# A hybrid decoder step: dt's columns and the sample's scores in strips, value products in pairs, the conv state in six pieces

## The chip, the cores and the metric

One NeuronCore of a Trainium2 chip runs the whole program. TensorE multiplies matrices into PSUM, VectorE and ScalarE work on rows of up to 128 partitions, GpSimd (POOL) and SyncE (SP) mainly issue DMAs, and 16 DMA engines move data between HBM and the on-chip memory. The metric is the time of one execution on the device, in microseconds (us), as the median of several runs.

## The reference

One layer of a decoder handles 256 prompt tokens and 8 sample tokens with the same weights: 264 columns in all.

```python
h = rmsnorm(x)
q, k, v, z, xbc, dt, qm, g = split(h @ w_in)      # 2048 -> 13856 features; dt has 32
A = sliding_window_attention(q, k, v)             # 16 heads, 4 key heads, window 128
B = mamba2_ssd(conv(xbc), z, softplus(dt + bias)) # 32 heads, state 128, conv over 4 tokens
M = attention(qm, memory)                         # 4 heads, 256 memory tokens
x = x + (sig(g_A)*(A @ up_A) + sig(g_B)*(B @ up_B) + sig(g_M)*(M @ up_M)) @ w_out
x = x + (silu(n @ w_gate) * (n @ w_up)) @ w_down  # n = rmsnorm(x)
```

A sample token attends to 128 cached keys of its own and to its own new key. Its convolution uses three cached tokens (`state_conv`, 8 x 3 x 3072). Keys, values and states are also outputs. Everything is float32.

## The kernel before

Activations lie with features on the partitions: a feature tile is 128 features by 264 tokens, and the 2048 features of h are 16 tiles. Weights come in units of 128 x 1024 numbers. For each unit SP issues a DMA into `raw`, ScalarE rounds it to `hi` in the matrix format float32r (L181, in `split`), VectorE takes the rest `lo = raw - hi` (L182), and TensorE multiplies (L160, in `mm`). A product in full precision is three matrix products: `hi` with the high part of the activation (`hh`), `hi` with its low part (`hl`), `lo` with the high part. An ordinary group gives 512 output features: eight units of 24 products each. `feed(i)` asks for the DMAs four units ahead and splits three units ahead.

The units stand in a list, and the loop at the end of the kernel runs through it. After each unit it lets two queues of side work go on: `side` with a credit of 1.0 for a unit, `slow` with 0.75. A task is a generator, and each `yield` gives the price of the step it has done; `yield None` ends the turn. `side` does its tasks in order: memory norm, `prep_x`, `consts`, memory attention, `swa_keys` (W1), `swa` (W), the convolutions of B and C, `task_dt`, and the four SSD groups. `side.drain(name)` finishes a task at once; `x_group(0)`, the unit group behind dt's, drains W first.

This is only the order of tracing. The tile framework then plans the order of each engine with a simulated timeline: what was traced earlier has precedence, and what is not ready in the simulation lets later work pass. On the chip each engine follows the planned order, and semaphores stop it where data is late.

Tiles come from pools. `sps` gives one of three PSUM tiles for side work, `dps` one of five for the groups; `t1`, `t2`, `t4` give SBUF tiles of 264, 512 and 1056 numbers, four each.

The places that the change touches:

- `consts` (L498 to L549) makes constants. The conv state comes as three DMAs of 24 rows (8 tokens x 3) by 1024 channels into `sc` (L535), and 24 transposes of 24 x 128 turn it into `scT`. VectorE multiplies by the conv weights and sums into `pre` (L541, L544). L518 makes a mask `m16` of row number modulo 16.
- `swa` (L821) is the window attention. It makes `qmask`, the sample's queries with zeros where key head and query head differ (L838 to L843), in the column order token, head pair, half, head. For each of four (block, pair of key heads) it computes scores and softmax, then the values: a piece is 128 keys for two query heads of each of two key heads, four transposes into `pT` (L923), a ScalarE copy into `pTa` (L925), and two float32 products into `po`, one into partitions 0 to 63 and one into 64 to 127 (L929). The later block has four pieces for a pair of key heads, the first block two.
- The sample scores follow (L938 on). For two tokens at a time four transposes turn the cached keys into `kcT`; for each token and pair of key heads one product with the keys stationary and 8 columns of `qmask` moving goes into `sTs`. VectorE copies it, a transpose puts it into `sS` with a row for each token and head, and one more product adds the new key's score. Then come softmax, transposes into `pSt`, a copy into `pTS`, and the value products `poS`, in strips of 32 output columns.
- `dt_group` (L1337) computes the 32 features of dt in two units, each with eight feature tiles of 128 weight columns: dt's 32 and 96 of the next part, which aren't used. It has 48 products into `pdt`.
- `task_dt` (L1106) transposes dt (`dtT`), adds the bias, and makes softplus, running sums and decay factors.

Of the kernel before, what the change touches and what calls it, by code (L numbers as in the profile page):

```python
# [18 lines left out]
P = 128  # L19
# [58 lines left out]
def tile_hybrid_decoder_step(  # L78
# [80 lines left out]
    def mm(out, lhsT, rhs, start=True, stop=True):  # L159
        nc.tensor.matmul(out, lhsT=lhsT, rhs=rhs, start=start, stop=stop)  # L160
# [91 lines left out]
    def do_split(n):  # L252
        if n < state["split"]:
            return
        raw = raws.pop(n)
        hi = wp.tile([P, 1024], F32R, tag="hi", name=nm("hi"), bufs=3)
        lo = wp.tile([P, 1024], F32R, tag="lo", name=nm("lo"), bufs=3)
        if units[n].get("perm"):
            for k in range(2):
                v = [t[:, k * 512:(k + 1) * 512].rearrange("p (r a d) -> p a r d", r=4, a=2) for t in (hi, lo)]  # L260
                s = raw[:, k * 512:(k + 1) * 512].rearrange("p (a r d) -> p a r d", a=2, r=4)
                split(v[0], v[1], s)
        else:
            split(hi, lo, raw)
        parts[n] = (hi, lo)
        state["split"] = n + 1
# [228 lines left out]
    def consts():  # L495
# [22 lines left out]
        V.tensor_reduce(m16, ident.rearrange("p (b h) -> p h b", h=16), axis=AX.X, op=ALU.add)  # L518
# [14 lines left out]
        for h in range(3):  # L533
            sc = t4("sc")[0:24, 0:1024]
            nc.gpsimd.dma_start(sc, state_conv[0, :, :, h * 1024:(h + 1) * 1024].rearrange("b k c -> (b k) c"))  # L535
            ps = sps("scT")
            for c in range(8):
                tr(ps[:, c * 24:(c + 1) * 24], sc[:, c * P:(c + 1) * P])
            tm = t1("tm")
            w3 = cw.rearrange("p (k c) -> p c k", k=4)[:, h * 8:(h + 1) * 8, 0:3]  # L540
            V.tensor_tensor(tm[:, 0:192].rearrange("p (c b k) -> p c b k", c=8, b=NS),  # L541
                            ps[:, 0:192].rearrange("p (c b k) -> p c b k", c=8, b=NS),
                            w3.unsqueeze(2).broadcast_to([P, 8, NS, 3]), op=ALU.mult)
            V.tensor_reduce(pre[:, h * 8:(h + 1) * 8, :], tm[:, 0:192].rearrange("p (c b k) -> p c b k", c=8, b=NS),  # L544
                            axis=AX.X, op=ALU.add)
            yield 1
# [274 lines left out]
    def swa():  # L821
# [16 lines left out]
        qm_ = t1("qmask")[:, 0:P].rearrange("p (b v a r) -> p b v a r", b=NS, v=2, a=2)  # L838
        V.memset(qm_.rearrange("p b v a r -> p (b v a r)"), 0.0)
        for a in range(2):  # L840
            rows = slice(a * 64, a * 64 + 64)
            for kvp in range(2):
                V.tensor_copy(qm_[rows, :, kvp, a, :].rearrange("p b r -> p r b"), q[rows, 4 * kvp:4 * kvp + 4, NP:NT])  # L843
        qmf = qm_.rearrange("p b v a r -> p (b v a r)")
# [31 lines left out]
        for blk in (1, 0):  # L876
            nk = 256 if blk else 128
            for kvp in range(2):
# [38 lines left out]
                for rp in range(2):  # L917
                    for kb in range(nk // P):
                        p2 = sps("pT")
                        for a in range(2):  # L920
                            for r2 in range(2):
                                o = (2 * a + r2) * P
                                tr(p2[:, o:o + P], s[a][:, 2 * rp + r2, kb * P:(kb + 1) * P])  # L923
                        pT = t2("pTa")
                        act(pT, p2, AF.Copy)  # L925
# [10 lines left out]
        pT_s = sps("sTs")  # L936
        kcs = {}
        for b in range(NS):  # L938
            if b % 4 == 0:
                kc = next(other_loads).rearrange("p (b c) -> p b c", b=4)  # L940
            if b % 2 == 0:
                ps = sps("kcT")
                for j in range(2):
                    for c in range(2):
                        tr(ps[:, (2 * j + c) * P:(2 * j + c + 1) * P], kc[:, b % 4 + j, c * P:(c + 1) * P])
                kcT = t2("kcT")
                act(kcT, ps, AF.Copy, scale=gq_c)
            for c in range(2):
                o = b * 16 + c * 8
                mm(pT_s[:, o:o + 8], kcT[:, (2 * (b % 2) + c) * P:(2 * (b % 2) + c + 1) * P], qmf[:, o:o + 8])  # L950
            yield 0.1
        sT = t1("sTsb")[:, 0:P]
        V.tensor_copy(sT, pT_s[:, 0:P])
        pkn = t1("pkn")[:, 0:P].rearrange("p (b v e) -> p b v e", b=NS, v=2)
        V.tensor_tensor(pkn, qm_.rearrange("p b v a r -> p b v (a r)"),
                        kT[:, :, NP:NT].rearrange("p v b -> p b v").unsqueeze(3).broadcast_to([P, NS, 2, 8]), op=ALU.mult)
# [27 lines left out]
        mm(ps[:, P:2 * P], ones, dg)  # L984
        pT = t1("pTS")[:, 0:256]
        V.tensor_copy(pT, ps[:, 0:256])
# [118 lines left out]
    def task_dt():  # L1105
# [34 lines left out]
        xs = tiny("dts", NS)[0:32]  # L1140
        V.tensor_scalar(xs, raw[:, NP:NT], hcol[:, 0:1], None, op0=ALU.add)
# [195 lines left out]
    def dt_group():  # L1337
        st = {}

        def loads(u):  # L1340
            def f(raw):
                return [(raw.rearrange("p (k n) -> p k n", k=8),
                         w_in[0, 8 * u * P:8 * (u + 1) * P, C_DT:C_DT + P].rearrange("(k p) n -> p k n", p=P))]
            return f

        def prod(u):
            def f(hi, lo):
                if u == 0:
                    st["ps"] = dps("pdt")[:, 0:NT]
                for k in range(8):  # L1350
                    kk = 8 * u + k
                    wh, wl = hi[:, k * P:(k + 1) * P], lo[:, k * P:(k + 1) * P]
                    mm(st["ps"], wh, hh(kk), start=kk == 0, stop=False)
                    mm(st["ps"], wh, hl(kk), start=False, stop=False)
                    mm(st["ps"], wl, hh(kk), start=False, stop=kk == KT - 1)
            return f

        def after():
            raw = t1("dtraw")[0:32]
            act(raw, st["ps"][0:32], AF.Copy)  # L1360
# [3 lines left out]
        for u in range(2):  # L1364
            units.append(dict(loads=loads(u), prod=prod(u), after=after if u else None))
# [310 lines left out]
```

## Time and profile before

| | |
|---|---|
| median of 3 runs | 1933.8 us (1928.26, 1933.8, 1938.96) |
| profiled execution | 1933.54 us, its span 1931.8 us |
| mean granted TensorE clock | 0.999 |
| DMA | 402.92 MB, mean 209 GB/s |
| costliest group, TensorE | the projection `pin`, 3 x 1728 products of 128 x 264 |

A line of the time order holds the start in us from the span's beginning, the time taken, the engine, the line of the kernel, the operation, what is written from what (out<-in), the shape (for a product, rows of contraction x output rows, then the moving operand) and how many instructions stand in it; in brackets follows the idle time before it and what ended it. PE is TensorE's products, PEld its weight loads. Matrix products overlap, so the times of single ones don't add up; from one start to the next does. A line of the waits holds who waited, for whom, the total, how many times, and the longest. In a list by tile three numbers are the shortest, median and longest time of one in ns.

### The profile page before, as it was taken

To read this page: it belongs to the slowest core of one execution; us is meant where nothing else is said; L and a number is where in the kernel's file an instruction comes from. 1 tells how busy PE (TensorE), PEld (TensorE's weight loads), DVE (VectorE), ACT (ScalarE), POOL (GpSimd) and SP (SyncE) were. 2 spreads that over 40 slices of the span, in tenths; PEclk is the share of its full clock that TensorE was granted. 3 is DMA by queue.
4 is the path that set the end of the run, shared out by engine and by line. 5 is a ranking of instruction groups with operands and counts; after the bars stand their busy time and mean duration, and the time that the engine had idled before them with its cause. 6 is when DMAs were issued, how large, how long until landed. Compare 5 with 4: busy or idle time off the path is not lost.

```text
span 1931.8 us, 37682 instructions
## 1 busy us (share of the span) xinstructions
PE 1905.2 (99%) x15401; PEld 1857.1 (96%) x15401; DVE 1168.0 (60%) x2246; ACT 969.7 (50%) x1423; POOL 133.6 (7%) x269
## 2 busy tenths in 40 slices
PE   8999999999999999999999999999999999999998
PEld 6899999989999999999999999999999999999998
DVE  5665577665568878588455666555445555445553
ACT  6654456665657685646444444444334434334443
POOL 3010101001002122011000000000000000000000
PEclk9999999999999999999999999999999999999999
DMA  8686758767668789778656656665556665566653
GB/s 278 209 264 214 212 171 297 223 190 234 200 181 279 241 228 301 250 262 282 180 189 213 222 182 176 184 182 180 183 178 183 178 185 177 184 177 183 176 192 126
DMA packets 191956, 402.92 MB, mean 209 GB/s; under 512 B 13891, under 2 KB 16242, under 8 KB 191648
## 3 DMA queue, kind: packets, MB, share of 16 engines
q1 hardware_dynamic: 169856, 324.13, 54.6%
q0 software_dynamic: 21776, 76.33, 11.9%
q8 instruction: 120, 1.97, 0.4%
q14 instruction: 52, 0.43, 0.1%
q10 hardware_dynamic: 152, 0.07, 0.0%
HBM read 376.53 MB, written 26.22 MB: 208 GB/s over the span
## 4 chain that ended last, share of the span: by engine, by line
PE 87%; DMA 4%; issue 4%; DVE 3%; ACT 2%; POOL 1%; ACTq 0%; SPq 0%; POOLq 0%; DVEq 0%
PE pin L160 25%; PE pu L160 13%; PE pdn L160 13%; PE pg L160 13%; PE pus L160 5%; PE pout L160 5%; PE pmem L160 5%; DMA ring<-in_state_ssm_dram 2%; PE pum L160 1%; PE pua L160 1%; DVE lo L182 1%; DMA ld<-in_cache_mem_v_dram 1%; DVE ring L1295 1%; DMA ld<-in_cache_mem_k_dram 1%; ACT hi L181 0%
## 5 line engine op out<-in xcount | busy, mean ns | idle before, releaser
L182 DVE TENSOR_TENSOR lo<-raw,hi 128x1024 fp32r<-128x1024 f32 (+1 forms) x626 | 746.8, 1196 | 599.4 <-ACT hi L181 598.2
L181 ACT ACTIVATE hi<-raw 128x1024 fp32r<-128x1024 f32 (+1 forms) x626 | 646.0, 1036 | 835.0 <-PE pin L160 191.8
L160 PE MATMUL pin<-hh,hi 128*128 128x264 f32 x1728 | 489.3, 287 | 0.6 <-DVE sig L1439 0.5
L160 PE MATMUL pin<-hl,hi 128*128 128x264 f32 x1728 | 489.0, 286 | 0.0
L160 PE MATMUL pin<-hh,lo 128*128 128x264 f32 x1728 | 473.8, 285 | 1.8 <-DVE lo L182 1.8
L160 PEld LDWEIGHTS pin<-hh,hi 128*128 128x128 f32 x1728 | 325.4, 189 | 5.6 <-issue 3.6
L160 PEld LDWEIGHTS pin<-hl,hi 128*128 128x128 f32 x1728 | 325.5, 188 | 2.7 <-issue 2.4
L160 PEld LDWEIGHTS pin<-hh,lo 128*128 128x128 f32 x1728 | 317.3, 188 | 3.8 <-DVE lo L182 2.3
L160 PE MATMUL pdn<-fah,hi 128*128 128x264 f32 x704 | 199.7, 285 | 0.0
L160 PE MATMUL pdn<-fal,hi 128*128 128x264 f32 x704 | 199.4, 285 | 0.0
L160 PE MATMUL pu<-h2h,hi 128*128 128x264 f32 x704 | 199.4, 284 | 0.0
L160 PE MATMUL pu<-h2l,hi 128*128 128x264 f32 x704 | 199.3, 284 | 0.0
L160 PE MATMUL pg<-h2l,hi 128*128 128x264 f32 x704 | 199.1, 285 | 0.0
L160 PE MATMUL pg<-h2h,hi 128*128 128x264 f32 x704 | 198.4, 284 | 0.0
L160 PE MATMUL pdn<-fah,lo 128*128 128x264 f32 x704 | 197.0, 284 | 0.0
L160 PE MATMUL pu<-h2h,lo 128*128 128x264 f32 x704 | 196.6, 284 | 0.0
L160 PE MATMUL pg<-h2h,lo 128*128 128x264 f32 x704 | 196.1, 284 | 0.0
L160 PEld LDWEIGHTS pdn<-fah,hi 128*128 128x128 f32 x704 | 132.7, 189 | 0.1
L160 PEld LDWEIGHTS pu<-h2h,hi 128*128 128x128 f32 x704 | 132.7, 189 | 0.0
L160 PEld LDWEIGHTS pg<-h2h,hi 128*128 128x128 f32 x704 | 132.7, 188 | 0.0
L160 PEld LDWEIGHTS pdn<-fal,hi 128*128 128x128 f32 x704 | 132.6, 188 | 0.1
L160 PEld LDWEIGHTS pu<-h2l,hi 128*128 128x128 f32 x704 | 132.6, 188 | 0.0
(531 smaller groups left out, 2966.0 us busy)
## 6 DMA issues: line engine op xcount, KB each, us to landing
raw<-in_w_in_dram SPq DMA_DIRECT2D x218, 512.0 KB, 4.3
raw<-in_w_gate_dram SPq DMA_DIRECT2D x88, 512.0 KB, 3.7
raw<-in_w_up_dram SPq DMA_DIRECT2D x88, 512.0 KB, 3.9
raw<-in_w_down_dram SPq DMA_DIRECT2D x88, 512.0 KB, 4.2
raw<-in_w_mem_kv_dram SPq DMA_DIRECT2D x32, 512.0 KB, 4.5
raw<-in_w_up_ssd_dram SPq DMA_DIRECT2D x32, 512.0 KB, 4.2
raw<-in_w_out_dram SPq DMA_DIRECT2D x32, 512.0 KB, 4.4
ld<-in_cache_mem_k_dram POOLq DMA_DIRECT2D x16, 512.0 KB, 5.8
```

Of the source, the lines that this page charges most:

```text
L160: nc.tensor.matmul(out, lhsT=lhsT, rhs=rhs, start=start, stop=stop)
L181: act(hi, src, AF.Copy)
L182: V.tensor_tensor(lo, src, hi.bitcast(F32), op=ALU.subtract)
L1295: V.scalar_tensor_tensor(hb, bb[:, b], dx[:, b:b + 1], hb, op0=ALU.mult, op1=ALU.add)
```

## The change

- **dt**: one unit instead of two. Its DMA takes only the 32 columns of dt, for all 16 feature tiles (2048 pieces of 128 bytes). Nothing is split: ScalarE copies the 512 columns, and the products are plain float32. Feature tiles 4j to 4j + 3 go into four strips of 32 partitions of `pdt`, so that the strips' sum is dt. `mm` returns its instruction, and `tc.keep_in_program_order` pins each of these products behind the one traced before it on TensorE.
- **`task_dt`** sums the four strips with a matrix `sm` of ones at equal row number modulo 32, in place of the transposes, and takes the sample's columns the same way.
- **Value products**: the pieces go in pairs, eight transposes and two copies first, then the eight products, the later piece first, pinned.
- **Sample scores**: `qmask` has a new column order, which separates even and odd tokens. The keys of all tokens are transposed first (two `t4` tiles). Then 16 float32 products have 32 columns of masked queries (`wq`, VectorE copies) stationary and 128 keys moving, in four strips, four deep, pinned, straight into `sS`. The copy `sTs` and the transpose go. Copying `pTS` restores the old column order in four pieces.
- **Conv state**: four DMAs put six pieces of 96 rows by 128 channels into `sc`; six transposes, two multiplications and two sums follow.
- `m16` gets the new row order.

```diff
@@ -157,7 +157,7 @@
     def mm(out, lhsT, rhs, start=True, stop=True):
-        nc.tensor.matmul(out, lhsT=lhsT, rhs=rhs, start=start, stop=stop)
+        return nc.tensor.matmul(out, lhsT=lhsT, rhs=rhs, start=start, stop=stop)
@@ -255,7 +255,9 @@
         lo = wp.tile([P, 1024], F32R, tag="lo", name=nm("lo"), bufs=3)
-        if units[n].get("perm"):
+        if units[n].get("whole"):
+            act(hi.bitcast(F32)[:, 0:512], raw[:, 0:512], AF.Copy)
+        elif units[n].get("perm"):
@@ -515,7 +517,10 @@
         m16 = tiny("m16", 16)
-        V.tensor_reduce(m16, ident.rearrange("p (b h) -> p h b", h=16), axis=AX.X, op=ALU.add)
+        m2 = tiny("m2", 64)
+        V.tensor_tensor(m2, ident[:, 0:64], ident[:, 64:P], op=ALU.add)
+        V.tensor_reduce(m16.rearrange("p (v e) -> p v e", v=2), m2.rearrange("p (v b e) -> p v e b", v=2, b=4),
+                        axis=AX.X, op=ALU.add)
@@ -530,19 +535,19 @@
-        for h in range(3):
-            sc = t4("sc")[0:24, 0:1024]
-            nc.gpsimd.dma_start(sc, state_conv[0, :, :, h * 1024:(h + 1) * 1024].rearrange("b k c -> (b k) c"))
+        sc = t4("sc")[0:96, 0:768].rearrange("p (i n) -> p i n", i=6)
+        for c in range(4):
+            nc.gpsimd.dma_start(sc[24 * c:24 * c + 24],
+                                state_conv[0].rearrange("b k (i c n) -> c (b k) i n", c=4, n=P)[c])
+        for h in range(2):
             ps = sps("scT")
-            for c in range(8):
-                tr(ps[:, c * 24:(c + 1) * 24], sc[:, c * P:(c + 1) * P])
...
-                            axis=AX.X, op=ALU.add)
+            for i in range(3):
+                tr(ps[:, i * 96:(i + 1) * 96], sc[:, 3 * h + i])
+            tm = t2("tm")[:, 0:288].rearrange("p (c b k) -> p c b k", c=12, b=NS)
+            w3 = cw.rearrange("p (k c) -> p c k", k=4)[:, h * 12:(h + 1) * 12, 0:3]
+            V.tensor_tensor(tm, ps[:, 0:288].rearrange("p (c b k) -> p c b k", c=12, b=NS),
+                            w3.unsqueeze(2).broadcast_to([P, 12, NS, 3]), op=ALU.mult)
+            V.tensor_reduce(pre[:, h * 12:(h + 1) * 12, :], tm, axis=AX.X, op=ALU.add)
@@ -835,13 +840,16 @@
             tr(psT[:, t], ss[:, t * P:(t + 1) * P])
-        qm_ = t1("qmask")[:, 0:P].rearrange("p (b v a r) -> p b v a r", b=NS, v=2, a=2)
-        V.memset(qm_.rearrange("p b v a r -> p (b v a r)"), 0.0)
+        qmf = t1("qmask")[:, 0:P]
+        qm_ = qmf.rearrange("p (o v b e) -> p o v b e", o=2, v=2, b=4)
+        V.memset(qmf, 0.0)
             for kvp in range(2):
-                V.tensor_copy(qm_[rows, :, kvp, a, :].rearrange("p b r -> p r b"), q[rows, 4 * kvp:4 * kvp + 4, NP:NT])
-        qmf = qm_.rearrange("p b v a r -> p (b v a r)")
+                for o in range(2):
+                    V.tensor_copy(qm_[rows, o, kvp, :, 4 * a:4 * a + 4].rearrange("p b r -> p r b"),
+                                  q[rows, 4 * kvp:4 * kvp + 4, NP + o:NT:2])
@@ -914,8 +922,10 @@
-                for rp in range(2):
-                    for kb in range(nk // P):
+                pieces = [(rp, kb) for rp in range(2) for kb in range(nk // P)]
+                for n in range(0, len(pieces), 2):
+                    pTs_ = []
+                    for rp, kb in pieces[n:n + 2]:
@@ -923,40 +933,46 @@
                         act(pT, p2, AF.Copy)
+                        pTs_.append(pT)
+                        yield 0.2
+                    for (rp, kb), pT in reversed(list(zip(pieces[n:n + 2], pTs_))):
                             kv = 2 * kvp + a
-                            mm(po[rows, 256 * rp:256 * rp + 256], v_tok[:, vb_, kv * 64:(kv + 1) * 64],
-                               pT[:, 256 * a:256 * a + 256], start=kb == 0, stop=kb == nk // P - 1)
-                        yield 0.4
+                            tc.keep_in_program_order(
+                                mm(po[rows, 256 * rp:256 * rp + 256], v_tok[:, vb_, kv * 64:(kv + 1) * 64],
+                                   pT[:, 256 * a:256 * a + 256], start=kb == nk // P - 1, stop=kb == 0))
-        pT_s = sps("sTs")
-        kcs = {}
-        for b in range(NS):
+        wq = t2("wq").rearrange("p (i s e) -> p i s e", i=4, s=4)
+        V.memset(wq.rearrange("p i s e -> p (i s e)"), 0.0)
+        for i in range(4):
+            V.tensor_copy(wq[:, i, :, 8 * i:8 * i + 8], qmf.rearrange("p (s b e) -> p s b e", s=4, b=4)[:, :, i])
+        kcT = [t4("kcT")[:, 0:1024].rearrange("p (i s k) -> p i s k", i=2, s=4) for _ in range(2)]
+        for b in range(0, NS, 2):
                 kc = next(other_loads).rearrange("p (b c) -> p b c", b=4)
-            if b % 2 == 0:
-                ps = sps("kcT")
...
-                        kT[:, :, NP:NT].rearrange("p v b -> p b v").unsqueeze(3).broadcast_to([P, NS, 2, 8]), op=ALU.mult)
+            ps = sps("kcT")
+            for j in range(2):
+                for c in range(2):
+                    tr(ps[:, (2 * j + c) * P:(2 * j + c + 1) * P], kc[:, b % 4 + j, c * P:(c + 1) * P])
+            act(kcT[b // 4][:, b // 2 % 2].rearrange("p s k -> p (s k)"), ps, AF.Copy, scale=gq_c)
+            yield 0.2
+        yield None
         ps = sps("sS")
-        tr(ps[:, 0:P], sT)
-        mm(ps[:, P:P + 1], pkn.rearrange("p b v e -> p (b v e)"), onec)
+        for i in (3, 2, 1, 0):
+            for st_ in range(4):
+                tc.keep_in_program_order(mm(ps[32 * st_:32 * st_ + 32, 0:P], wq[:, i, st_], kcT[i // 2][:, i % 2, st_],
+                                            start=i == 3, stop=i == 0))
+        pkn = t1("pkn")[:, 0:P].rearrange("p (o v b e) -> p o v b e", o=2, v=2, b=4)
+        for v in range(2):
+            V.tensor_tensor(pkn[:, :, v], qm_[:, :, v],
+                            kT[:, v, NP:NT].rearrange("p (b o) -> p o b", o=2).unsqueeze(3).broadcast_to([P, 2, 4, 8]),
+                            op=ALU.mult)
+        mm(ps[:, P:P + 1], pkn.rearrange("p o v b e -> p (o v b e)"), onec)
@@ -982,8 +998,12 @@
         mm(ps[:, P:2 * P], ones, dg)
         pT = t1("pTS")[:, 0:256]
-        V.tensor_copy(pT, ps[:, 0:256])
+        for w in (0, P):
+            for o in range(2):
+                V.tensor_copy(pT[:, w:w + P].rearrange("p (b o v e) -> p o v b e", b=4, o=2, v=2)[:, o],
+                              ps[:, w:w + P].rearrange("p (o v b e) -> p o v b e", o=2, v=2, b=4)[:, o])
@@ -1108,9 +1128,16 @@
         x = tiny("dtx", 64)
+        sm = t1("dtsum")[:, 0:P]
+        V.tensor_reduce(sm[:, 0:32], ident.rearrange("p (a h) -> p h a", a=4), axis=AX.X, op=ALU.add)
+        V.tensor_copy(sm[:, 32:P].rearrange("p (a h) -> p a h", a=3), sm[:, 0:32].unsqueeze(1).broadcast_to([P, 3, 32]))
         for t in range(2):
-            tr(ps[:, t * 32:(t + 1) * 32], raw[:, t * P:(t + 1) * P])
+            mm(ps[:, t * 32:(t + 1) * 32], raw[:, t * P:(t + 1) * P], sm[:, 0:32])
+        mm(ps[:, 64:64 + NS], sm, raw[:, NP:NT])
+        xs = tiny("dts", NS)[0:32]
+        V.tensor_scalar(xs, ps[0:32, 64:64 + NS], hcol[:, 0:1], None, op0=ALU.add)
@@ -1137,8 +1164,6 @@
-        xs = tiny("dts", NS)[0:32]
-        V.tensor_scalar(xs, raw[:, NP:NT], hcol[:, 0:1], None, op0=ALU.add)
@@ -1335,34 +1360,29 @@
     def dt_group():
-        st = {}
-        def loads(u):
...
-            return f
+        def loads(raw):
+            return [(raw[:, 0:512].rearrange("p (k n) -> p k n", k=KT),
+                     w_in[0, :, C_DT:C_DT + 32].rearrange("(k p) n -> p k n", p=P))]
+        def prod(hi, lo):
+            ps = dps("pdt")[:, 0:NT]
+            w = hi.bitcast(F32)
+            for j in range(4):
+                for x in (hh, hl):
+                    for q in range(4):
+                        k = 4 * j + q
+                        tc.keep_in_program_order(mm(ps[32 * q:32 * q + 32], w[:, 32 * k:32 * k + 32], x(k).bitcast(F32),
+                                                    start=j == 0 and x is hh, stop=j == 3 and x is hl))
+            ssd["dtps"] = ps
         def after():
-            raw = t1("dtraw")[0:32]
-            act(raw, st["ps"][0:32], AF.Copy)
+            raw = t1("dtraw")
+            act(raw, ssd["dtps"], AF.Copy)
-        for u in range(2):
-            units.append(dict(loads=loads(u), prod=prod(u), after=after if u else None))
+        units.append(dict(loads=loads, prod=prod, after=after, whole=True))
     mg = {}
```

More of the change, by code (lines that the diff above doesn't have):

```diff
@@ L531, in consts @@
         yield 3
-        for h in range(3):
-            sc = t4("sc")[0:24, 0:1024]
-            nc.gpsimd.dma_start(sc, state_conv[0, :, :, h * 1024:(h + 1) * 1024].rearrange("b k c -> (b k) c"))
-            ps = sps("scT")
-            for c in range(8):
-                tr(ps[:, c * 24:(c + 1) * 24], sc[:, c * P:(c + 1) * P])
[L539 to L544, printed above, removed]
-                            axis=AX.X, op=ALU.add)
+        sc = t4("sc")[0:96, 0:768].rearrange("p (i n) -> p i n", i=6)
[3 more added lines that the diff above has]
+        for h in range(2):
+            ps = sps("scT")
+            for i in range(3):
[5 more added lines that the diff above has]
+            V.tensor_reduce(pre[:, h * 12:(h + 1) * 12, :], tm, axis=AX.X, op=ALU.add)
             yield 1
@@ L939, in swa @@
             if b % 4 == 0:
                 kc = next(other_loads).rearrange("p (b c) -> p b c", b=4)
-            if b % 2 == 0:
-                ps = sps("kcT")
[L943 to L955, printed above, removed]
-                        kT[:, :, NP:NT].rearrange("p v b -> p b v").unsqueeze(3).broadcast_to([P, NS, 2, 8]), op=ALU.mult)
-        ps = sps("sS")
-        tr(ps[:, 0:P], sT)
-        mm(ps[:, P:P + 1], pkn.rearrange("p b v e -> p (b v e)"), onec)
+            ps = sps("kcT")
@@ L1337, in dt_group @@
     def dt_group():
-        st = {}
-        def loads(u):
-            def f(raw):
-                return [(raw.rearrange("p (k n) -> p k n", k=8),
-                         w_in[0, 8 * u * P:8 * (u + 1) * P, C_DT:C_DT + P].rearrange("(k p) n -> p k n", p=P))]
-            return f
[L1346 to L1356, printed above, removed]
+        def loads(raw):
[11 more added lines that the diff above has]
+            ssd["dtps"] = ps
         def after():
-            raw = t1("dtraw")[0:32]
-            act(raw, st["ps"][0:32], AF.Copy)
+            raw = t1("dtraw")
+            act(raw, ssd["dtps"], AF.Copy)
             ssd["dtraw"] = raw
             side.ready.add("dt")
-        for u in range(2):
-            units.append(dict(loads=loads(u), prod=prod(u), after=after if u else None))
+        units.append(dict(loads=loads, prod=prod, after=after, whole=True))
     mg = {}
```

## Prediction

> **What bounds the kernel now.** I read the page's head first, then the list of TensorE's waits, then the instructions in order of time around the four places that the change touches.
>
> ```profile
> PE 1905.2 (99%) x15401; PEld 1857.1 (96%) x15401; DVE 1168.0 (60%) x2246; ACT 969.7 (50%) x1423; POOL 133.6 (7%) x269
> ```
>
> TensorE is the bound, and no other engine is above 60%. The profiled execution took 1933.54 us, 1.7 us more than its span of 1931.8; the median of the three runs is 1933.8 us, so the sum below can be set against either. They run from 1928.26 to 1938.96 us, and I take about 0.5% (9.7 us) as the least that a measurement of this kernel can tell from no change.
>
> ```profile
> PE pv L164 <- DMA vg<-in_norm_mix_dram: 7.0, 1, 7.0
> PE pua L160 <- ACT sig L1434: 3.8, 2, 2.6
> PE memT L164 <- DMA ring<-in_mem_prompt_dram: 2.5, 1, 2.5
> PE pin L160 <- DVE lo L182: 1.8, 2, 1.0
> PE pmT L164 <- DVE pm L674: 1.7, 2, 1.3
> PE oms L160 <- DMA ld<-in_cache_mem_v_dram: 1.6, 1, 1.6
> PE xtok L164 <- ACT xs L1037: 1.2, 1, 1.2
> PE pua L160 <- ACT hi L181: 0.8, 1, 0.8
> PE pin L160 <- DVE sig L1439: 0.5, 1, 0.5
> PE dsc L160 <- DVE ex L1148: 0.4, 1, 0.4
> ```
>
> These are all the waits of TensorE that the profile shows: who waited, for whom, us in total, times, the longest. Two belong to the start (7.0 and 2.5); the other eight sum to 11.8 us. So a change here acts in two ways: it shortens TensorE's own row of instructions, and it moves those 11.8 us. No wait in the list is one of the products that are rewritten: what they cost is issue time.
>
> Busy time doesn't give that cost, since instructions overlap. The step from one start to the next does:
>
> ```profile
> 435.91 0.28 PE L160 MATMUL pin<-hh,lo 128*128 128x264 f32 x1
> ...
> 438.97 0.28 PE L160 MATMUL pin<-hh,hi 128*128 128x264 f32 x1
> 439.10 0.95 PE L160 MATMUL sTs<-qmask,kcT 128*128 128x8 f32 x8
> 439.90 0.64 PE L164 MATMUL kcT<-ident,ring 128*128 128x128 f32 x4
> 440.30 0.37 PE L160 MATMUL pin<-hl,hi 128*128 128x264 f32 x1
> 440.50 0.28 PE L160 MATMUL pin<-hh,lo 128*128 128x264 f32 x1
> ```
>
> From 435.91 to 438.97 are 25 steps: 0.122 us for a full-width product of 264 columns. The eight sample score instructions take 439.10 to 439.90, 0.80 us, or 0.10 each for 8 columns. Coming back from such work, the first product's step is 0.20, 0.08 over the usual one.
>
> **The change, part by part.**
>
> *dt.* Removed: 16 feature tiles with three products each, 48 x 0.122 = 5.86 us.
>
> ```profile
> 464.10 0.28 PE L160 MATMUL pin<-hh,lo 128*128 128x264 f32 x1
> 464.31 1.07 PE L160 MATMUL poS<-ring,pTS 128*32 128x256 f32 x16
> 465.31 0.39 PE L160 MATMUL pin<-hh,hi 128*128 128x264 f32 x1
> 465.53 0.28 PE L160 MATMUL pin<-hl,hi 128*128 128x264 f32 x1
> 475.66 0.64 PE L160 MATMUL oms<-ld,pb 128*32 128x256 f32 x8
> 476.23 0.30 PE L164 MATMUL dtT<-ident,dtraw 32*128 32x32 f32 x2
> 476.46 0.39 PE L160 MATMUL pin<-hl,hi 128*128 128x264 f32 x1
> ```
>
> poS is the form that dt takes: plain float32, 32 output columns, four strips, two instructions for each call (16 for the kernel's 8 calls). Sixteen take 464.31 to 465.31, 1.00 us; eight take 475.66 to 476.23, 0.57. The difference prices eight, two sets of four strips: 0.43, so 0.215 for a set and 0.14 fixed. Going in costs 464.31 - 464.10 - 0.12 = 0.09, coming out 465.53 - 465.31 - 0.12 = 0.10. dt now has 32 calls, 64 instructions, 16 sets of 264 columns: 16 x 0.215 x 264/256 = 3.55, with 0.14 + 0.09 + 0.10 it is 3.88. **Gain 1.98 us.** If side work is put between its sets, each break costs some 0.3 (0.14 + 0.09 + 0.10); nothing to three of these are the ends.
>
> *Sample scores.* Removed: four times 0.80 and a transpose at 0.10, with one return of 0.08: 3.38. The transposes of the cached keys stay. Added: 16 calls, 32 instructions, 8 sets of four strips with 128 columns. The nearest row has 128 columns in two strips:
>
> ```profile
> 516.74 1.09 PE L160 MATMUL py<-dec,xdt 128*64 128x128 f32 x16
> 517.77 0.49 PE L160 MATMUL cb<-CT,BT 128*128 128x128 f32 x2
> ```
>
> That is 8 sets in 1.03 us, ends included. With the two changes of form it is 1.22. Above, the set of 256 columns bounds it: 8 x 0.215 + 0.33 = 2.05. I take 1.22, the row with its column count. **Gain 2.15** (1.3 to 2.2).
>
> *Value products in pairs.*
>
> ```profile
> 324.87 0.65 PE L160 MATMUL po<-pTa,v_tok 128*64 128x256 f32 x4
> 325.45 1.09 PE L164 MATMUL pT<-ident,s 128*128 128x128 f32 x8
> 326.30 0.37 PE L160 MATMUL pin<-hl,hi 128*128 128x264 f32 x1
> ```
>
> One piece is four instructions: 0.58 from its start to that of the transposes behind it, with the 0.09 in and the 0.08 out of the rows above 0.75. There are 12 pieces (eight of the later block, four of the first), 9.0 us. A pair puts two more sets of 0.22 into one excursion: 0.58 + 0.44 + 0.17 = 1.19; six are 7.14. **Gain 1.86.** Below, nothing, if the planner had to break up each pair. The pinned order ties a pair's first product to the second copy: behind it in TensorE's queue stands everything the planner put later, pin products mostly, and ScalarE and VectorE wait for those in turn.
>
> *Conv state.*
>
> ```profile
> 113.80 1.67 PE L164 MATMUL scT<-ident,sc 24*128 24x24 f32 x24
> 115.40 0.39 PE L160 MATMUL pin<-hh,hi 128*128 128x264 f32 x1
> 115.62 0.28 PE L160 MATMUL pin<-hl,hi 128*128 128x264 f32 x1
> L535 POOL DMA_DIRECT2D sc<-in_state_conv_dram x3: 501/519/528, 21.3 to 22.3; - x3
> ```
>
> The 24 transposes take 113.80 to 115.40, 1.60 us, and 0.10 out; with 0.09 in, as for the strips (they fill 24 rows of the array), 1.79. Six with 96 rows take 6 x 0.106 (pT above: 0.85 for 8) and one return of 0.08: 0.72. **Gain 1.07.** Four DMAs of 0.52 us issue stand on POOL's queue for three, with pieces of 512 bytes for 4 KB; they are issued at 21 us and read at 113, so even ten times the landing time would be hidden.
>
> *dt's later task.* Two transposes of 0.23 (476.23 to 476.46) become three float32 calls with 128 stationary columns, six instructions at 0.11 (the sample scores had 0.10): 0.66, and a return of 0.09 of its own. **Loss 0.5.**
>
> *VectorE and ScalarE.* Removed: two `lo` splits and two `hi` copies of 1024 columns, for one copy of 512, and a unit of the weight queue. Added: some fourteen small VectorE operations (the scores' blocks, their mask, the reordering of the probabilities, dt's summing matrix). At 0.15 to 0.3 us they are as much as the two splits. I cost them at nothing, as TensorE has products of the projection to do meanwhile; without that cover they would be about 3 us. One place has no cover:
>
> ```profile
> 275.53 0.58 DVE L843 COPY qmask<-qT 64x32 f32<-64x32 f32 x4
> 285.52 0.39 PE L160 MATMUL pin<-hh,lo 128*128 128x264 f32 x1 [0.97 <-DVE lo L182]
> ```
>
> Four copies become eight of half the size, and ten microseconds on TensorE waits 0.97 for a `lo` of VectorE. If VectorE is full in between, the wait grows by what the copies add. The cost lies between 0 and another 0.58; I take 0.4, nearer to the row.
>
> *dt's load.*
>
> ```profile
> dtb_bc<-in_dt_bias_dram POOLq DMA_DIRECT2D x1, 16.0 KB, 8.6
> ```
>
> One DMA with 2048 pieces of 128 bytes replaces two with 1024 of 512. No row shows such a weight load; the nearest is this one, 128 pieces of 128 bytes, which landed in 8.6 us. Weights are asked for four units ahead, 4 x 24 x 0.122 = 11.7 us. Nothing is one bound; the other, if it lands in twice 8.6, is 5.5 us of waiting. I take nothing, since the row lies within the lead.
>
> **Sum**: 1.98 + 2.15 + 1.86 + 1.07 - 0.5 - 0.4 = 6.16. 1933.54 - 6.16 = **1927.4 us**, 0.3% faster, less than can be told from no change. The last 1070 us (the feed-forward part and the outputs) aren't touched.
>
> **The rivals.**
>
> *The moved waits shrink* (chance 0.2). The window part ends a few us sooner, and the waits after 430 us (pua 3.8 and 0.8, oms 1.6, xtok 1.2, sig 0.5, dsc 0.4: 8.3) are set by the new plan. For it: the rewritten work stands ahead of all of them. Against: none waits for it. Half gone gives 1923, all gone 1919.
>
> *The pair's copy is late* (0.12, the one that ends slower). Place: a pair's first value product. The planner takes the second copy as done; on the chip the copy of 0.60 us stands behind a `hi` copy of 1.04, and TensorE stands 1.64 us. Six times is 9.8: 1937.2. From the fourth pair on (6.16 / 1.64) the kernel is slower than before. For it: the score tiles share three PSUM slots, `po` and two pieces fill them, and `oms` holds one from 374 to 488 us, so the second piece must wait for the first.
>
> ```profile
> L925 ACT ACTIVATE pTa<-pT x12: 574/597/602, 321.8 to 427.4; 128x512 f32<-128x512 f32 x12
> L181 ACT ACTIVATE hi<-raw x7: 1040/1047/1064, 414.6 to 436.6; 128x1024 fp32r<-128x1024 f32 x7
> L160 PEld LDWEIGHTS poS<-ring,pTS x16: 106/110/110, 464.3 to 464.8; 128*32 128x32 f32 x16
> ```
>
> Against: po has no row among the waits now, with the same copy in front.
>
> *The strips don't overlap* (0.03), so the change doesn't do what it says: each set's four weight loads, 0.11 each in the last row, stand ahead of its products. Then a set costs 0.44 more; 16 + 8 sets cost 10.6, and the time is 1937.9. Against: poS's 16 loads and products together took 1.00 us, where this would need 2.8. [...]
>
> The forecast's own case has 0.6, 1923.5 to 1932 us: within it dt broken up, scores at 2.05 and waits moved by some 3 us either way. The last 0.05 is a new wait elsewhere, at the gates of the window part's up-projection most likely, where the longest one (2.6) is now.
>
> Range 1918 to 1937 us: it takes in the first two rivals but for their ends. Faster by over 0.5% (below 1924.1): most of the first rival and the forecast's edge with the measurement's spread, 0.28. Slower by over 0.5% (above 1943.5): only several rivals together, 0.05. Within: 0.67.
>
> **What would show it.** In the trace after: pdt as 64 instructions in some 3.9 us; sS as 32 in about 1.2 and no sTs; po in six excursions of eight; scT with six; and TensorE's waits (without the start) at 8 to 16 us. It is wrong if po appears among the waits, if pdt's sets lie more than 0.3 us apart, or if the waits at pua or xtok grow by more than the 6 us saved.

## The result, and the profile after

| | before | after |
|---|---|---|
| median | 1933.66 us (4 runs, 1928.26 to 1938.96) | 1949.03 us (4 runs, 1946.17 to 1950.95) |
| profiled span | 1931.8 us | 1948.9 us |
| mean granted TensorE clock | 0.999 | 0.997 |

The ratio is 1.0084, with a 95% interval of 1.0058 to 1.0110: 16 us slower, where 6 us faster was forecast. The time lies outside the range that was stated (1918 to 1937 us).

The products that were rewritten are where and as they were forecast. From the time order of TensorE after:

```profile
113.33 0.41 PE L164 MATMUL scT<-ident,sc 96*128 96x96 f32 x3
113.52 0.37 PE L160 MATMUL pin<-hh,hi 128*128 128x264 f32 x1
...
327.57 1.08 PE L160 MATMUL po<-pTa,v_tok 128*64 128x256 f32 x8
328.59 1.09 PE L164 MATMUL pT<-ident,s 128*128 128x128 f32 x8
...
424.71 1.08 PE L160 MATMUL sS<-kcT,wq 128*32 128x128 f32 x32
425.72 0.38 PE L160 MATMUL sS<-ones,pkn 128*128 128x1 f32 x2
...
439.52 0.63 PE L160 MATMUL pdt<-hh,hi 128*32 128x264 f32 x8
439.97 0.63 PE L160 MATMUL pdt<-hl,hi 128*32 128x264 f32 x8
...
443.19 0.39 PE L160 MATMUL pin<-hh,hi 128*128 128x264 f32 x1
```

Read it from start to start. A pair of value pieces takes 1.02 us. The sample's 32 score instructions take 1.01. Eight instructions of dt, which are two sets of strips, take 0.45, and all 64 take 3.67, unbroken. Adding up these steps for all rewritten products, after minus before: scores -2.15, dt -2.48, conv state -1.21, value products -0.91 (without what the fewer returns save their neighbours), dt's later task +0.27 to +0.54: about 6.3 us less. So the loss lies elsewhere. TensorE's waits after (who, for whom, us in total, times, longest):

```profile
PE pv L164 <- DMA vg<-in_norm_mix_dram: 8.3, 1, 8.3
PE ssy L160 <- ACT sqy L1280: 4.8, 1, 4.8
PE pin L160 <- DVE lo L182: 4.3, 6, 1.2
PE pua L160 <- ACT sig L1454: 4.2, 4, 2.7
PE pin L160 <- ACT hi L181: 3.7, 4, 1.4
PE pua L160 <- ACT hi L181: 2.5, 2, 1.5
...
PE pT L164 <- DVE s L921: 1.7, 1, 1.7
```

Without the two waits of the start they sum to 28.4 us, against 11.8 before. `ssy` is the row sum behind an SSD group, `pua` the up-projection of the window part. Where they lie is shown by the view by stretches, whose columns are the stretch, its length, then busy time and instructions of TensorE, its weight loads, VectorE, ScalarE and POOL, then clock, DMA share and GB/s. Before, and then after:

```profile
300.00:570.00 270.00, 267.95 (x2276) 250.70 (x2275) 175.49 (x404) 169.53 (x300) 21.39 (x38) 1.00 0.68 214
570.00:780.00 210.00, 202.72 (x1726) 198.89 (x1725) 171.24 (x492) 143.49 (x249) 46.92 (x67) 0.99 0.87 266
```

```profile
300.00:570.00 270.00, 263.05 (x2258) 242.25 (x2257) 175.67 (x417) 166.14 (x297) 22.68 (x40) 1.00 0.67 210
570.00:780.00 210.00, 193.22 (x1622) 187.94 (x1621) 161.09 (x477) 134.09 (x232) 44.83 (x64) 0.98 0.81 241
```

From 570 to 780 us, where no product was rewritten, TensorE does 104 instructions fewer in the same time. Setting the k-th product of the main groups beside the same one before: it is 3.1 us late at 317 us, 0.2 at 536, behind the rewritten products, then 9.1 at 611, 15.7 at 667, and 17.4 at 905, which stays to the end. From 570 to 780 us the states of the sample (`state_ssm`, 32 loads of 256 KB) stream through the core, beside the weights. One place of it, first ScalarE's time order after, with the idle time and what ended it in brackets:

```profile
723.45 1.28 ACT L1319 ACTIVATE ring<-ring,dsc 128x128 f32<-128x128 f32 x4 [4.47 <-DMA ring<-in_state_ssm_dram]
730.08 0.40 ACT L1319 ACTIVATE ring<-ring,dsc 128x128 f32<-128x128 f32 x1 [5.35 <-DMA ring<-in_state_ssm_dram]
730.39 1.04 ACT L1280 ACTIVATE sqy<-y 128x1024 f32<-128x1024 f32 x1
...
731.92 1.04 ACT L181 ACTIVATE hi<-raw 128x1024 fp32r<-128x1024 f32 x1
...
733.16 0.92 ACT L1454 ACTIVATE sig<-pin 128x264 f32<-128x264 f32 x3
```

and TensorE's at the same place:

```profile
731.48 1.08 PE L160 MATMUL ssy<-sqy,ones 128*32 128x64 f32 x32 [4.84 <-ACT sqy L1280]
733.58 0.59 PE L160 MATMUL pua<-aTh,hi 128*128 128x264 f32 x1 [1.01 <-ACT sig L1454]
```

ScalarE does its list in order here: it stands 4.47 and 5.35 us at L1319, where it scales a state by its decay, because the state hasn't landed. Behind that instruction in its list stand `sqy`, a `hi` copy of weights, and the gate `sig`, all of whose inputs are there: VectorE has finished `y`, which `sqy` reads, at 723.83 us, in the line below; the last `pin` product ends at 725.9 us and the weights have landed by 727.6. Behind those three stands TensorE, 4.84 us at `ssy` and 1.01 at `pua`.

```profile
722.60 1.23 DVE L1278 TENSOR_TENSOR y<-y,z 128x1024 f32<-128x1024 f32 x1
```

The chain of waits names the load that ends it:

```profile
721.23 8.77 DMA ring<-in_state_ssm_dram
```

In the whole of after ScalarE waits 30.1 us for states, 14 times, against 18.9 and 12 before. The line of before, and then that of after:

```profile
ACT ring L1294 <- DMA ring<-in_state_ssm_dram: 18.9, 12, 3.4
```

```profile
ACT ring L1319 <- DMA ring<-in_state_ssm_dram: 30.1, 14, 5.4
```

### The profile page after: what moved, and what is told of

Same layout as the page of the kernel before. It is cut to its first block, busy times and chain, and to the rows that moved or that the text cites. A ratio compares the mean times of both kernels' runs of the same rounds, so it can differ in the third digit from the quotient of the medians.

```text
span 1948.9 us, 37693 instructions
## 1 busy us (share of the span) xinstructions
PE 1906.7 (98%) x15402; PEld 1853.8 (95%) x15402; DVE 1168.6 (60%) x2257; ACT 969.6 (50%) x1423; POOL 135.4 (7%) x270
## 4 chain that ended last, share of the span: by engine, by line
PE 60%; DVE 2%; ACT 2%; DMA 1%; issue 1%; POOL 0%; ACTq 0%; DVEq 0%; POOLq 0%
PE pu L160 13%; PE pdn L160 13%; PE pg L160 13%; PE pin L160 9%; PE pus L160 5%; PE pout L160 5%; PE pua L160 1%; DMA ring<-in_state_ssm_dram 1%; PE pum L160 1%; DVE lo L182 1%; ACT hi L181 0%; ACT dec L1255 0%; DVE jkh L1321 0%; DMA mgi<-mg_d 0%; ACT ring L1319 0%
```

## The experiments

**What was asked first.** The change has a second effect, beside the rewritten work: it shifts the turns of the side tasks. dt is one unit instead of two, so `side` and `slow` lose one turn. The price of a piece of value products falls from 0.4 to 0.2 while there are as many pieces, so a turn's credit buys more of the window part. And a `yield None` ends one turn. Counting the turns through both programs in units of the weight list of before, the window part ends two units earlier, the convolution of C one, and the first stream of states begins at unit 154 for 156. From unit 185 on the tasks of `side` are level again, since they then wait for products of the main list; the streams of states, which stand in `slow`, stay two units ahead for three of the four groups. So: is it the turns, or the work? Three kernels put the turns back, moved them alone, and put prices and pause back but not dt's turn, which makes the tasks a unit later than before.

e1, the changed kernel with the turns of before:

```diff
-                        yield 0.2
+                        yield 0.4
...
-        yield None
...
-        side.step(SIDE_US)
-        slow.step(SLOW_US)
+        for _ in range(2 if u.get("whole") else 1):
+            side.step(SIDE_US)
+            slow.step(SLOW_US)
```

> All of the change stays, but the side queue's turns fall as before: the value pieces give a price of 0.4 again, the pause ahead of the scores goes, and the single dt unit is followed by two turns of side and slow work, so that every task from C on starts at the same unit as in the kernel before. Theory T (turns): the rewritten products saved about 6 us as forecast, and the loss of some 21 us in waits between 570 and 780 us comes from side tasks that start one to two units earlier against the gate and up-projection groups; then this kernel takes 1925 to 1930 us, with pua's waits near 4.6 us. Rival W (work): the pinned products, pairs and strips themselves cause the waits; then it stays at 1945 to 1952 us.

1931.62 us, 1.0011 (0.9998 to 1.0023). The loss is gone, but the time is above the 1925 to 1930 us expected: the 6 us of the rewritten work don't show.

e2, the kernel before with the turns of after and nothing else:

```diff
-                        yield 0.4
+                        yield 0.2
...
+        yield None
...
-            units.append(dict(loads=loads(u), prod=prod(u), after=after if u else None))
+            units.append(dict(loads=loads(u), prod=prod(u), after=after if u else None, dt=True))
...
-        side.step(SIDE_US)
-        slow.step(SLOW_US)
+        if not (u["after"] is None and u.get("dt")):
+            side.step(SIDE_US)
+            slow.step(SLOW_US)
```

> The kernel before, with none of the rewritten work, but with the turns of the changed one: value pieces at 0.2, a pause ahead of the scores' end, and no turn after the first dt unit, so that each task from C on starts at the unit where it starts in the changed kernel. Theory T: 1948 to 1957 us, slower than before by the waits alone, with waits at pua and ssy. Rival W: 1931 to 1936 us, no different from before.

1946.69 us, 1.0084 (1.0069 to 1.0099), just below the time expected, at after's ratio: the whole loss, with not one product rewritten. Its longest waits are at the places of after's:

```profile
PE pua L160 <- ACT hi L181: 5.7, 3, 3.2
PE ssy L160 <- ACT sqy L1256: 4.2, 1, 4.2
...
PE pua L160 <- ACT sig L1435: 1.9, 3, 1.4
```

and its stretch is like after's, with 1607 instructions of TensorE:

```profile
570.00:780.00 210.00, 193.58 (x1607) 188.04 (x1606) 159.76 (x472) 134.98 (x235) 43.15 (x61) 0.97 0.81 240
```

Here the products are those of before, so the account can be closed. e2's profiled span is 13.9 us longer than before's. Its waits behind the start sum to 20.4 us for 11.8, 8.6 more; and TensorE works 12.0 us at half clock for 3.4 (the last section), which is some 4.3 us of work lost: 12.9 together.

e3, the changed kernel with prices and pause as before, but one turn for dt (the change of price and the pause in e1's edit):

> The changed kernel with the prices of the value pieces as before and no pause, but one dt unit with one turn: the tasks from C on start one unit later than in the kernel before, counted by the weights. Theory T says only that it differs from the changed kernel, since the turns lie two units apart: 1925 to 1942 us. Rival W: 1945 to 1952 us.

1924.80 us, 0.9978 (0.9968 to 0.9988): faster than both kernels. e4, the changed kernel with the second turn after dt alone (the lines on `step` in e1's edit), which leaves the prices low and puts the tasks one more unit ahead:

> The changed kernel with a second turn after the dt unit and nothing else: the tasks from C on start one more unit earlier than in the changed kernel. Theory T, if earlier is worse: 1950 to 1958 us; if it is a matter of where a task meets a gate group, anything from 1926 to 1958. Rival W: 1945 to 1952 us.

1941.56 us, 1.0052 (1.0037 to 1.0068). It is bad too, but not worse than after: the loss doesn't grow with every unit.

**What of the turns does it.** e5 is the kernel before without the turn after dt's first unit, so with the turns of e3:

> The kernel before with one turn of side and slow work less (none after the first dt unit), and nothing else: its tasks from C on start at the same units as in e3_yields_back, one later than before. If the turns alone made e3 fast and the rewritten work is worth nothing, this is about 0.998 of before too (1924 to 1929 us). If the work's 6 us come through once no wait takes them, this is 6 us slower than e3: 1929 to 1934 us.

1926.74 us, 0.9989 (0.9977 to 1.0000). The next two move nothing but the streams of states, by the price that each SSD group's sample part pays at its head (L1310 in the kernel after). e6 is after with 4.5 for 3.0, states later; e7 is before with 1.5 for 3.0, states earlier:

```diff
-        yield 3.0
+        yield 4.5
```

> The changed kernel with one number changed: the price of the first step of each group's sample state task is 4.5 for 3.0, so that its loads start two to four units later, as in the kernel before, while all side tasks stay where the change put them. Theory S (of the turns, it is the state stream that matters: ScalarE stands in order at state tiles whose DMAs land late, and the gates' copies and the weight copies behind it release TensorE late): most of the 15 us come back, 1930 to 1938 us, and ssy's and pua's waits shrink. Rival V (the side tasks' own work against the gates matters): it stays at 1942 to 1952 us.

> The kernel before with the same price at 1.5 for 3.0: the state loads start one to three units earlier, all side tasks stay. Theory S: slower than before, 1938 to 1950 us. Rival V: 1928 to 1936 us.

e6 took 1936.59 us, 1.0032 (1.0020 to 1.0044): of the 16 us, 10 come back. e7 took 1939.40, 1.0057 (1.0035 to 1.0079): 11 us lost by that one number. So the place of the states in the order is by itself worth some ten us. How much of the 16 us is theirs isn't settled, since neither kernel moves them by just what the change did. Counted by the turns, the first state of the four groups is taken up at units 157, 182, 207 and 240 before, at 155, 180, 205 and 240 after; in e6 at 157, 184, 211 and 242, in e7 at 156, 178, 201 and 239, further than was expected of them. And e6, with its states about where e3 has them or later (158, 183, 208 and 240 there), is still 10 us above e3 by the ratios. That points to the early turns of the other side tasks as a second part, but no run moves those alone. e7's profile, 4.7 us longer than before's, has only 0.6 us of waits at `ssy` and 1.6 at `pua`; it doesn't show the chain of after. ScalarE's waiting in e6 warns against reading the amount of its waiting as the cost:

```profile
PE pin L160 <- DVE lo L182: 5.5, 8, 1.3
...
PE ssy L160 <- ACT sqy L1280: 0.4, 1, 0.4
```

It still waits 29.6 us for states there, yet TensorE's wait at `ssy` is 0.4 for 4.8 and `pua` has left the list: as much waiting stands ahead of work that TensorE doesn't wait for. Its stretch shows it, with 1728 instructions, where before has 1726:

```profile
570.00:780.00 210.00, 202.34 (x1728) 197.37 (x1727) 169.06 (x489) 141.66 (x246) 46.27 (x66) 1.00 0.84 258
```

**Where the 6 us went.** With equal turns the rewritten work was worth nothing that can be told from noise: e1 against before +0.11%, e3 against e5 -0.11%, after against e2 0.00%. In all of these kernels with the rewritten work, and in none without, TensorE lost 2.4 to 4.9 us between 300 and 317 us, counted by the k-th product. VectorE's time order in e3 has two idle times there, and POOL's the cause of the first:

```profile
305.07 0.43 DVE L710 CUSTOM_DVE_ANT_0 jks<-ld,qb 128x256 f32<-128x256 f32 x1 [1.88 <-DMA qb<-qd]
314.67 0.16 DVE L918 TENSOR_TENSOR dena<-dena,es 128x4 f32<-128x4 f32 x1 [2.34 <-ACT s L916]
```

```profile
297.29 0.53 POOL L596 DMA_DIRECT2D ld<-in_cache_mem_k_dram  x1 [7.62 <-DVE rs_y L862]
297.81 1.05 POOL L705 DMA_DIRECT2D qb<-qd  x2
```

`qb` is a broadcast of one sample token's memory query. Two go out together here, behind a load that waits for `rs_y`; before, the first goes out 7.75 us ahead of the second:

```profile
291.75 0.53 POOL L700 DMA_DIRECT2D qb<-qd  x1
...
299.50 0.53 POOL L700 DMA_DIRECT2D qb<-qd  x1
```

Of the rewritten work only one thing stands just ahead of it on VectorE: the eight copies into `qmask`, for four. So e9 is e3 with four copies in the new column order, e10 the same with the turns of before, and e11 the kernel before with its four copies cut into eight:

```diff
-                for o in range(2):
-                    V.tensor_copy(qm_[rows, o, kvp, :, 4 * a:4 * a + 4].rearrange("p b r -> p r b"),
-                                  q[rows, 4 * kvp:4 * kvp + 4, NP + o:NT:2])
+                V.tensor_copy(qm_[rows, :, kvp, :, 4 * a:4 * a + 4],
+                              q[rows, 4 * kvp:4 * kvp + 4, NP:NT].rearrange("p r (b o) -> p o b r", o=2))
```

> e3 (the changed kernel with the prices of before, no pause and one turn after dt) with the sample's queries put into qmask by four VectorE copies, as before, for eight; the columns stay in the new order. Theory Q: the eight copies make VectorE late ahead of the window's scores, the sixth of the broadcasts qb then goes out behind one more load on POOL's queue, about 8 us later, and TensorE waits some 3 us more between 300 and 315 us (1.7 of them for s at pT). Undone, the sixth qb is issued some 8 us ahead of the seventh again, the wait at pT goes, and the time is about 3 us below e3's: 0.9955 to 0.9970 of before. Rival: the copies lie beside products, the wait has another cause or is only moved, and the time stays within 1 us of e3's, 0.9973 to 0.9983.

> e1 (the changed kernel with prices, pause and turns as before) with the four copies in place of eight. Theory Q: 3 us below e1, 0.9990 to 1.0000 of before, with no wait of TensorE for s at pT near 310 us. Rival: as e1, 1.0005 to 1.0015.

> The kernel before with eight copies of half the size into qmask in place of four, in its own column order: nothing else. Theory Q: the sixth qb goes out next to the seventh, TensorE waits 2 to 3 us more between 300 and 315 us, and the kernel takes 1.0010 to 1.0020 of before. Rival: no change, 0.9995 to 1.0005.

e9 took 1919.94 us, 0.9954 (0.9941 to 0.9967), 4.6 us below e3's ratio; e10 1928.92, 0.9995 (0.9984 to 1.0005), 3.1 below e1's; e11 1937.11, 1.0041 (1.0027 to 1.0054), 8 us above before. The intervals leave some 3 us either way on each of these differences, so that e10's alone is hardly clear of noise. The order on POOL turns with the copies, in e9 and then in e11:

```profile
289.08 0.53 POOL L705 DMA_DIRECT2D qb<-qd  x1
294.95 0.53 POOL L596 DMA_DIRECT2D ld<-in_cache_mem_k_dram  x1 [5.34 <-DVE scs L710]
295.47 0.53 POOL L705 DMA_DIRECT2D qb<-qd  x1
```

```profile
302.32 0.53 POOL L591 DMA_DIRECT2D ld<-in_cache_mem_k_dram  x1 [7.64 <-DVE rs_y L855]
302.84 1.05 POOL L700 DMA_DIRECT2D qb<-qd  x2
```

In e11, where nothing but the copies was cut, the two `qb` go out together as in e3. It is so in every profile, e12's below included: together in all six kernels with eight copies, apart in all seven with four. The copies themselves are a trifle, eight in e11 and four in e9:

```profile
278.18 0.84 DVE L844 COPY qmask<-qT 64x16 f32<-64x16 f32 x8
```

```profile
272.81 0.58 DVE L850 COPY qmask<-qT 64x32 f32<-64x32 f32 x4
```

0.26 us more on VectorE, and 3 to 8 us more at the end, through the order that the planner then chose. e11's loss is more than twice what was expected: its profile has 2.9 us of it between 300 and 317 us, and 2.7 ahead of 242 us, which is ahead of the copies; there a single wait of the memory attention at `pmT` is 3.6 us, for 1.3 before. The rest isn't placed.

e9 is the fastest kernel. TensorE's waits in it, apart from the start, sum to 5.1 us:

```profile
PE pin L160 <- DVE lo L182: 2.4, 3, 1.0
PE pin L160 <- ACT hi L181: 1.0, 1, 1.0
...
```

Last, are the two causes apart? e12 is the changed kernel with the four copies and nothing else.

> The changed kernel with four copies into qmask in place of eight, and nothing else: its turns stay one unit early. If the two causes are apart and add up (eight copies 3 to 5 us as in e9 and e10, the early turns the rest), it is 3 to 5 us below the changed kernel: 1.0058 to 1.0069 of before, with the waits for hi, sig and sqy between 570 and 780 us still there and none for s at pT near 310 us. Rival: without the late window part the early turns do no harm, and it comes to 0.997 to 1.000.

1944.82 us, 1.0073 (1.0054 to 1.0091). The early turns do the harm by themselves, so the rival falls, and `ssy` waits 4.6 us as in after, while `pT` waits no more. But only 2 us came back for the 3 to 5 expected; by the two intervals it is anything from 4 us lost to 8 gained. Whether the causes add up is open.

The ratios in one table, by the turns and by the work:

| turns of the side tasks | work of before | rewritten, eight copies | rewritten, four copies |
|---|---|---|---|
| as after | 1.0084 (e2) | 1.0084 (after) | 1.0073 (e12) |
| as before | 1 | 1.0011 (e1) | 0.9995 (e10) |
| a unit later | 0.9989 (e5) | 0.9978 (e3) | 0.9954 (e9) |

Down a column is what the turns do, up to 1.2%. Along a row is what the work does: with four copies and the latest turns 0.35%, or 6.8 us (some 3 us either way, by the two intervals), the size that was forecast, though with four copies and in the latest turns alone.

## Why the prediction was wrong

- **The bound.** Right: TensorE stays the bound, busy for 1906.7 us of the span of 1948.9, and no rewritten product stands in the list of waits.
- **dt, scores, conv state.** Right. The forecast had 3.88 us for dt's products, 1.22 for the scores and 0.72 for the conv state; the new rows give 3.67, 1.01, and with returns of 0.1 about 0.6. In their own steps dt gained 2.48 for 1.98, the scores 2.15 for 2.15, the conv state 1.21 for 1.07.
- **Value products in pairs.** Right as to form: six excursions of eight, 1.02 us each in the row above, which is the forecast's 0.58 + 0.44. In their own steps they gained 0.91; the other 0.95 of the 1.86 were returns, which lie in the neighbours' steps and can't be told from moved waits.
- **dt's later task.** -0.5 forecast, -0.27 to -0.54 measured. **dt's load at nothing**: right, no wait for it in the list.
- **VectorE's qmask copies.** Mis-sized. The step "I take 0.4, nearer to the row" was bounded by the copies' own 0.58 us. Four copies for eight were worth 4.6, 3.1 and 2.1 us in three pairs of kernels (the last not clear of noise), and eight for four cost 8 us in the fourth: they turn the order of a load and a broadcast on POOL.
- **The step that failed.** It stands in the paragraph on VectorE and ScalarE: "a unit of the weight queue" was listed among what is removed, and "I cost them at nothing". A unit less is a turn less, and the prices in the `yield`s, which stood in the diff, weren't costed at all. e2 has the cost of just that, with the pause: 16 us. The front part of this document says that what is traced earlier has precedence; the prediction's sum took TensorE's order as fixed and priced the instructions in it.
- **The rivals.** The late copy of a pair: refuted, `po` is in no list of waits. Strips that don't overlap: refuted again, since dt's 64 weight loads, of 0.11 us each, and its 64 products took 3.67 us together, where the loads alone come to 7.0. Moved waits: they moved, but grew, by 16.6 us (28.4 less 11.8). The last 0.05, "a new wait elsewhere, at the gates of the window part's up-projection", named the place: `pua` has 7.0 us of waits for 4.6, and the wait at `ssy` is new. It had no price and no mechanism.
- **What would show it.** One line told the failure: TensorE's waits without the start were to be 8 to 16 us and are 28.4. The line on `pua` and `xtok` was too narrow: together they grew from 5.8 to 7.0 us in the list of waits, and the loss was spread over `ssy`, `pin` and `pua`.

The account of the 17.1 us between the two spans: 16.6 more waiting, some 2.2 from the clock (below), less 6.3 of the products, 12.5; the other 4.6 aren't placed. Single executions of before lie up to 13 us apart (1925.67 to 1938.96), so a few us between two profiles can be noise.

What stays open: why starting the states two units earlier costs the most (e4, one more unit ahead, loses less than after); how much of the loss is the states' and how much the other side tasks'; and why the work is worth 6.8 us a unit late but only 1 us at the turns of before (e10 against before). Set product by product against before, e10 is 2.9 us ahead at 300 us, 8.1 at 536 and 1.1 at 780: the saving is there ahead of the states' stretch and lost in it, while e9 is 2.7, 10.3 and 14.3 us ahead at the same places. In e10 TensorE has waits of 4.7 us at `pua` behind the same copies and gates on ScalarE, which e9 hasn't. That time saved on TensorE ahead of such a chain only makes the wait longer fits this, but no run here was made to show it.

## What to carry to other kernels

Where a planner orders the engines from the order of tracing, price what an edit does to that order before the instructions: every unit, turn, price or pause that it adds or drops moves all side tasks behind it, and here that was worth up to 1.2% where the instructions were worth 0.35%. Look then for the engine that does its list in order and waits for a late DMA: here what counted was not how long it waited (ScalarE 30.1 us for states in after, 29.6 in e6) but who stood behind it (TensorE, 4.8 us at `ssy` in after, 0.4 in e6). And measure a rewrite with the schedule held equal, by putting the turns back, before judging it.

## What the runs showed of the hardware

Late in some waits, or behind them, TensorE's granted clock was 0.50 here, for 3.4 or 6.8 us, so that such a wait cost more than its own length. In after the longer stretch begins at 730.4 us, 1.1 us before the 4.84 us wait ends. Behind that wait, from the time order of after:

```profile
733.96 0.42 PE L160 MATMUL pua<-aTl,hi 128*128 128x264 f32 x1
734.18 0.42 PE L160 MATMUL pua<-aTh,lo 128*128 128x264 f32 x1
...
738.24 0.28 PE L160 MATMUL pua<-aTh,hi 128*128 128x264 f32 x1
738.36 0.28 PE L160 MATMUL pua<-aTl,hi 128*128 128x264 f32 x1
```

A step takes 0.22 us at first and 0.12 later, with the granted clock beside it:

```profile
734.00:736.00 2.00, 2.00 (x11) 2.00 (x11) 1.49 (x4) 1.98 (x4) 0.00 (x0) 0.50 0.34 43
738.00:740.00 2.00, 2.00 (x19) 2.00 (x18) 2.00 (x9) 0.65 (x1) 1.14 (x2) 1.00 0.77 268
```

By the clock's records after has two such stretches of 3.4 and 6.8 us, before one of 3.4, all at 0.5. TensorE works for 7.8 us of them after and for 3.4 before: 4.4 us more at half speed, so some 2.2 us of work lost. Not every wait brings one: in after none follows the 2.7 us wait at `pua` (623 us), while the stretch at 590.5 us follows waits of 1.0 and 1.2 us; and e6 has none, with 17.9 us of waits behind the start. Which waits bring one isn't shown.
